# A decoder layer on one core: named slots for transposed tiles, heads in other places among the matmuls, modulation blocks requested a step ahead

## The chip, the cores and the metric

One core of one Trainium2 chip runs the whole kernel. The metric is device time in microseconds (us) of one execution; the median of several runs counts. TensorE (PE) multiplies, VectorE (DVE) and ScalarE (ACT) work on vectors, GpSimd (POOL) makes masks, and SyncE (SP) issues most transfers from memory.

## The reference

One layer on 256 tokens of width 2048, in float32:

```
mod = silu(c) @ w_ada + b_ada              # six pieces: shift, scale, gate, twice
h   = rmsnorm(x) * (1 + s1) + sh1
p   = h @ w_in                             # 2048 x 6160: DA q,k,v; GLA q,k,v,gate, low rank
DA  : 8 heads, softmax(q1 k1) - lam * softmax(q2 k2), causal, ALiBi, then norm
GLA : 4 heads, o_t = q_t S_t,  S_t = diag(a_t) S_(t-1) + k_t v_t, norm, gated
x   = x + g1 * (concat(DA, GLA) @ w_o)
h2  = rmsnorm(x) * (1 + s2) + sh2
x   = x + g2 * ((gelu(conv3(h2 @ w_gate)) * (h2 @ w_val)) @ w_down)   # d_ff = 5632
out = rmsnorm(x) * g_final
```

## The kernel before

Each float32 product is made of three matmuls on a high and a low part of both operands. A unit is two k-tiles (of 128 rows) by 512 columns of a weight, 512 KB: `load_unit` (L110) requests it on SyncE (L122), ScalarE writes the high part `wh` (L125), VectorE the low part `wl` (L126), and TensorE makes 24 matmuls of 256 columns (`b_block`, L144) or 12 of 512 (`a_block`, L178).

The stages in order of time:
1. Start: x is transposed, its norm made, and the modulation of the first two k-tiles.
2. Input projection, in K groups of 2, 2, 4, 4, 4 k-tiles; each group goes over twelve blocks of 512 columns. A block that was begun in an earlier group is copied back into PSUM (L744) and out again (L749).
3. Output projection w_o. It takes the k-tiles 8 to 15 (GLA's heads, `mixT[4]` to `mixT[7]`) first and 0 to 7 (the DA heads, `mixT[0]` to `mixT[3]`) after them.
4. w_up, its K in groups of 4, 4 and 8 k-tiles, then w_down and the last norm.

Beside the units runs other work, written as generators. Background: the modulation blocks (`ada_gen`, L222) request rows of `w_ada` (L243, L246) and add them up on VectorE, weighted by the column of c (`acc`, L256); when a block is full, TensorE sums over partitions (`ps_mod`, L236) and `mod_cols` makes shift and scale (L268 to L271). Then `norm_gen` makes the tiles `hT` (`norm_T`, L281: high part L292 or L296, low part L297). Each unit gives the background a number of steps, `R_K`, `R_WO`, `R_SP`, `R_UP`. Foreground: the GLA heads (`gla`, L683) and the DA heads (`da`, L687), `F_GLA` and `F_DA` steps a unit. A third generator, `setup_consts` (L351), makes masks and constants with casts on VectorE (L374, L401, L415).

A DA head on TensorE is `ps_s` (scores, L577 and L579), `ps_pd` (transposes of the softmax, L607) and `ps_od` (the product with v, L613 to L615). `gla_T` (L553) and `da_T` (L630) transpose the heads' results into `mixT`; `gla_T` is called four times after the whole input projection. Tiles for `hT`, `mixT`, GLA's decay tiles `W` and others come from one pool of eight equal buffers under one name, in turn; PSUM tiles named `ms` have four buffers.

`raw_tile` (L103) gives a buffer for a weight: in the first part a ring of six; from w_up on four `raw2` buffers and four `late` ones, which lie in memory that the first part used. The order of instructions on each engine is that of a scheduler, which takes the program order and its own estimate of times; `keep_in_program_order` fixes an instruction behind the one ahead of it on its engine.

## Time and profile before

| | us |
|---|---|
| three runs | 1346.63, 1340.09, 1338.14 |
| median | 1340.09 |
| profiled execution | 1342.89 |
| its span in the trace | 1341.2 |
| TensorE busy | 1260.1 |
| VectorE busy | 882.0 |
| ScalarE busy | 723.8 |

A busy TensorE may be at its full clock or at half of it; the granted clock of a stretch stands beside its busy time. In brackets behind a row of a timeline stands how long the engine was idle before it, and what ended that.

### The profile page before, as it was taken

How to read it: one execution, taken by the hardware profiler on the slowest of the kernel's cores; microseconds unless marked ns; L12 is line 12 of the kernel's file. 1: busy time of each engine (PE TensorE's matmuls, PEld its weight loads, DVE VectorE, ACT ScalarE, POOL GpSimd, SP SyncE). 2: the span in 40 equal slices, each digit the busy share in tenths (PEclk: the TensorE clock that was granted, in tenths of full speed). 3: DMA queues.
4: the chain of work that ended last, by engine and by line, in shares of the span. 5: the costliest groups of instructions: out<-in, count | busy, mean ns of one | idle time of the engine just before them, and what ended most of it. 6: DMA issues, size and time to landing. Idle time of an engine off the chain costs nothing.

```text
span 1341.2 us, 21471 instructions
## 1 busy us (share of the span) xinstructions
PE 1260.1 (94%) x8556; PEld 1164.6 (87%) x8556; DVE 882.0 (66%) x1135; ACT 723.8 (54%) x937; POOL 30.6 (2%) x79
## 2 busy tenths in 40 slices
...
GB/s 279 298 362 341 307 280 347 268 215 193 177 216 128 201 241 114 180 366 285 285 260 318 237 223 246 231 225 157 210 235 233 233 251 192 173 197 191 190 197 102
DMA packets 159827, 314.58 MB, mean 235 GB/s; under 512 B 12045, under 2 KB 20941, under 8 KB 159726
## 3 DMA queue, kind: packets, MB, share of 16 engines
...
q14 instruction: 34, 0.28, 0.1%
...
## 4 chain that ended last, share of the span: by engine, by line
PE 64%; DMA 19%; DVE 8%; ACT 4%; issue 3%; POOL 2%; DVEq 0%; SPq 0%; POOLq 0%; ACTq 0%
PE ps_h L144 36%; PE ps_d L178 18%; DMA raw_a<-in_w_ada_dram 16%; DVE wl L126 4%; PE ps_mm L144 3%; PE ps_o L144 3%; DVE acc L256 2%; ACT wh L125 2%; DMA raw<-in_w_o_dram 1%; PE ps_mm L178 1%; DMA late<-in_w_up_dram 1%; PE ps_mod L865 1%; DMA late<-in_w_ada_dram 0%; DMA raw<-in_w_in_dram 0%; PE ps_s L579 0%
## 5 line engine op out<-in xcount | busy, mean ns | idle before, releaser
L125 ACT ACTIVATE wh<-raw 128x1024 fp32r<-128x1024 f32 x327 | 344.6, 1057 | 348.9 <-PE ps_d L178 121.4
L126 DVE TENSOR_TENSOR wl<-raw,wh 128x1024 fp32r<-128x1024 f32 x327 | 397.9, 1222 | 194.1 <-ACT wh L125 193.4
L144 PE MATMUL ps_h<-h2T,wh 128*128 128x256 f32 x2816 | 511.5, 285 | 8.1 <-ACT wh L125 8.0
L144 PEld LDWEIGHTS ps_h<-h2T,wh 128*128 128x128 f32 x2816 | 441.9, 193 | 8.2 <-ACT wh L125 8.2
L144 PE MATMUL ps_h<-h2T,wl 128*128 128x256 f32 x1408 | 400.8, 285 | 3.2 <-DVE wl L126 3.2
L256 DVE SCALAR_TENSOR_TENSOR acc<-raw_a,cols,acc 128x1024 f32<-128x1024 f32 (+1 forms) x161 | 192.1, 1194 | 127.5 <-DMA raw_a<-in_w_ada_dram 126.7
L144 PEld LDWEIGHTS ps_h<-h2T,wl 128*128 128x128 f32 x1408 | 271.8, 193 | 4.3 <-DVE wl L126 4.3
L178 PE MATMUL ps_d<-wh,act 128*128 128x512 f32 x704 | 218.1, 390 | 0.8 <-DVE dx L999 0.8
L178 PEld LDWEIGHTS ps_d<-wh,act 128*128 128x128 f32 x704 | 132.2, 188 | 29.5 <-DVE dx L999 1.2
L144 PE MATMUL ps_mm<-hT,wh 128*128 128x256 f32 x768 | 144.1, 289 | 13.2 <-ACT ps_mm L744 5.8
L178 PE MATMUL ps_d<-wl,act 128*128 128x512 f32 x352 | 137.9, 392 | 0.0
L144 PEld LDWEIGHTS ps_mm<-hT,wh 128*128 128x128 f32 x768 | 123.2, 196 | 15.1 <-ACT ps_mm L744 6.6
L178 PE MATMUL ps_mm<-wh,hT 128*128 128x512 f32 x384 | 125.7, 399 | 1.9 <-ACT pj_gq L749 0.6
L144 PE MATMUL ps_mm<-hT,wl 128*128 128x256 f32 x384 | 110.4, 288 | 0.0
L144 PE MATMUL ps_o<-mixT,wh 128*128 128x256 f32 x512 | 98.1, 292 | 7.2 <-DVE mixT L464 5.1
L125 ACT ACTIVATE wh<-late 128x1024 fp32r<-128x1024 f32 x65 | 68.2, 1054 | 58.1 <-PE ps_h L144 35.8
L126 DVE TENSOR_TENSOR wl<-late,wh 128x1024 fp32r<-128x1024 f32 x65 | 79.0, 1221 | 26.7 <-ACT wh L125 23.4
L144 PEld LDWEIGHTS ps_o<-mixT,wh 128*128 128x128 f32 x512 | 82.8, 198 | 8.7 <-DVE mixT L464 5.3
L178 PEld LDWEIGHTS ps_mm<-wh,hT 128*128 128x128 f32 x384 | 73.3, 191 | 19.4 <-ACT ps_mm L744 1.6
L178 PE MATMUL ps_mm<-wl,hT 128*128 128x512 f32 x192 | 76.4, 398 | 2.8 <-DVE wl L126 2.8
L178 PEld LDWEIGHTS ps_d<-wl,act 128*128 128x128 f32 x352 | 66.1, 188 | 14.1 <-issue 0.7
L144 PEld LDWEIGHTS ps_mm<-hT,wl 128*128 128x128 f32 x384 | 75.2, 196 | 0.4 <-issue 0.3
...
## 6 DMA issues: line engine op xcount, KB each, us to landing
raw_a<-in_w_ada_dram SPq DMA_DIRECT2D x142, 512.0 KB, 5.0
raw<-in_w_up_dram SPq DMA_DIRECT2D x111, 512.0 KB, 4.6
raw<-in_w_in_dram SPq DMA_DIRECT2D x96, 512.0 KB, 5.5
raw<-in_w_down_dram SPq DMA_DIRECT2D x88, 512.0 KB, 4.4
late<-in_w_up_dram SPq DMA_DIRECT2D x65, 512.0 KB, 4.9
raw<-in_w_o_dram SPq DMA_DIRECT2D x32, 512.0 KB, 4.8
late<-in_w_ada_dram SPq DMA_DIRECT2D x30, 512.0 KB, 4.4
raw_a<-in_w_ada_dram SPq DMA_DIRECT2D x32, 256.0 KB, 4.8
```

The source lines that it names most:

```text
L125: A.activation(h, raw, AF.Copy)
L126: V.tensor_tensor(l, raw, h, op=ALU.subtract)
L144: PE.matmul(ps[:, m * T:(m + 1) * T], w[:, j, ms], xt[k][:, xx, :], start=(first and k == kts[0] and m % 2 == 0 and i == 0), stop=(last an ...
L178: PE.matmul(ps[:, tb * 512:(tb + 1) * 512], xt[k][:, xx, tsl], w[:, j, :], start=(first and k == kts[0] and i == 0), stop=(last and k == k ...
L256: V.scalar_tensor_tensor(acc, raw[:, j], col, acc, op0=ALU.mult, op1=ALU.add)
L865: PE.matmul(ps_p[:, i:i + 1], pe_rows[k][:, i // 4, i % 4 * P:(i % 4 + 1) * P], cols[:, CK + k:CK + k + 1], start=(k == PE_ROWS[0] and i = ...
```

## The change

- The modulation block of the third K group (4 k-tiles) becomes two of 2 k-tiles, each with its norm (`ADA1`); the input projection drains them half by half. The steps a unit (`R_K`, `R_UP`) and of the DA heads (`F_DA`) are set anew.
- `ada_gen` requests each row one step before it adds it, so each block takes one step more. Its adds, the setup casts and some setup transfers stay in program order; the end of a block and the norms have high priority.
- The pool of eight buffers gets a name for each. GLA's results go into the slots of the decay tiles `W`, and `gla_T` is called inside `gla()`, for heads 0 and 1 after the step of head 2 and for 2 and 3 after the step of head 3, instead of after the input projection.
- `raw_tile` gives the four `raw2` buffers first and the `late` ones after them.
- `spill_o` and `pe_rows` change buffers.

```
+ADA1 = ((2,), (2,), (2, 2), (4,), (4,))
-R_K, R_WO, R_SP, R_UP = (0.95, 1.65, 0.85, 1.1, 0.7), 1.0, 0.75, 0.27
-F_GLA, F_DA = 2.3, 1.8
+R_K, R_WO, R_SP, R_UP = (0.95, 1.85, 0.88, 1.15, 0.75), 1.0, 0.75, 0.28
+F_GLA, F_DA = 2.3, 1.5
...
-    ktp = ctx.enter_context(tc.tile_pool(name="ktp", bufs=8))
+    ktp = ctx.enter_context(tc.tile_pool(name="ktp", bufs=1))
...
         if spare:
-            turn[0] = (turn[0] + 1) % (RAW[0] + len(spare))
-            if turn[0] < len(spare):
-                return spare[turn[0]].rearrange("p (a b) -> p a b", a=shape[1])
+            turn[0] = turn[0] % (RAW[0] + len(spare)) + 1
+            if turn[0] > RAW[0]:
+                return spare[turn[0] - RAW[0] - 1].rearrange("p (a b) -> p a b", a=shape[1])
...
-        for kt in range(0, rows, per):
+        pin = tc.keep_in_program_order
+
+        def load(kt):
             raw = raw_tile([P, per, n], "raw_a")
...
+            return raw
+
+        ahead = load(0)
+        yield
+        for kt in range(0, rows, per):
+            raw, ahead = ahead, load(kt + per) if kt + per < rows else None
...
-                    V.scalar_tensor_tensor(acc, raw[:, j], col, acc, op0=ALU.mult, op1=ALU.add)
+                    pin(V.scalar_tensor_tensor(acc, raw[:, j], col, acc, op0=ALU.mult, op1=ALU.add))
...
-        finish(acc if by_rows else ps)
+        with tc.high_priority():
+            finish(acc if by_rows else ps)
...
-            V.tensor_copy(cmat[:, l], cf)
+            pin(V.tensor_copy(cmat[:, l], cf))
...
-            Wt.append([ktp.tile([P, 4, NTB, P], F32, tag="kt", name=f"W{hd}{i}") for i in range(2)])
+            Wt.append([ktp.tile([P, 4, NTB, P], F32, tag=f"kt{4 + 2 * hd + i}", name=f"W{hd}{i}") for i in range(2)])
...
-        mixT[4 + hd] = kt_tile(f"mixT{4 + hd}")
+        mixT[4 + hd] = kt_tile(f"mixT{4 + hd}", 4 + hd)
...
-        n, k0 = len(kts), kts[0]
-        bg.append(("ada1", ada_gen((0, 1), n * P, k0 * P, mod_cols(s1, sh1, 0, GM, k0, n), get_ps,
-                                   FIRST_PE if g == 0 else ())))
-        bg.append((f"norm{g}", norm_gen(kts)))
+        k0 = kts[0]
+        for n in ADA1[g]:
+            bg.append(("ada1", ada_gen((0, 1), n * P, k0 * P, mod_cols(s1, sh1, 0, GM, k0, n), get_ps,
+                                       FIRST_PE if g == 0 else ())))
+            bg.append((f"norm{k0}", norm_gen(list(range(k0, k0 + n)))))
+            k0 += n
...
             yield from both(*([gla_b(hd - 1)] if hd else []), *([gla_a(hd)] if hd < GLA_HEADS else []))
 
+            for t in {3: (0, 1), 4: (2, 3)}.get(hd, ()):
+                gla_T(t)
+                yield
...
-    steps(5)
+    steps(6)
...
         for i, ks in enumerate(halves):
+            drain(f"norm{ks[0]}")
...
     while len(fg) > 1:
         fstep()
-    for hd in range(GLA_HEADS):
-        gla_T(hd)
     fg.append(da(1))
```

The order of instructions on VectorE at the start, before, from the end of the first modulation block (L268 to L271 make its shift and scale, L297 is the low part of the first `hT`):

```order
36 L365 TENSOR_TENSOR neglam<-lam_136 128x1
37 L256 SCALAR_TENSOR_TENSOR acc<-raw_a,cols,acc 128x512
38 L268 TENSOR_TENSOR sh_131<-ps_mod,bcol 128x2
39 L269 TENSOR_TENSOR s_130<-ps_mod,bcol 128x2
40 L401 CAST cmat<-cf 128x128
41 L366 TENSOR_SCALAR neglam<-neglam 128x1
42 L256 SCALAR_TENSOR_TENSOR acc<-raw_a,cols,acc 128x512
43 L271 SCALAR_TENSOR_TENSOR s_130<-s_130,cols 128x2
44 L401 CAST cmat<-cf 128x128 x2
45 L126 TENSOR_TENSOR wl<-raw,wh 128x1024
47 L401 CAST cmat<-cf 128x128 x2
48 L297 TENSOR_TENSOR hT_293<-xv,hT_293 128x256
```

The same place in the new order (L278 is L268, L281 is L271, L307 is L297, L127 is L126, L265 is L256):

```order
27 L265 SCALAR_TENSOR_TENSOR acc<-raw_a,cols,acc 128x512 x3
28 L374 TENSOR_TENSOR dlam<-dlam 128x128
29 L375 TENSOR_REDUCE lam_136<-dlam 128x2
30 L278 TENSOR_TENSOR sh_131<-ps_mod,bcol 128x2
31 L279 TENSOR_TENSOR s_130<-ps_mod,bcol 128x2
32 L127 TENSOR_TENSOR wl<-raw,wh 128x1024
33 L281 SCALAR_TENSOR_TENSOR s_130<-s_130,cols 128x2
34 L377 TENSOR_TENSOR neglam<-lam_136 128x1
35 L378 TENSOR_SCALAR neglam<-neglam 128x1
36 L307 TENSOR_TENSOR hT_293<-xv,hT_293 128x256
37 L127 TENSOR_TENSOR wl<-raw,wh 128x1024
38 L307 TENSOR_TENSOR hT_293<-xv,hT_293 128x256
```

The casts and the adds of the next block, which stood among them, are no longer there; one `wl` stands between L279 and L281.

TensorE before, from the last heads of DA(0) to the first matmuls of w_o (`ps_o` of L144; `ps_t` are GLA's transposes):

```order
1401 L607 MATMUL ps_pd<-ident,pt 128x128 x2
1402 L613 MATMUL ps_od<-pj_dv_151,pdT 128x128
1403 L614 MATMUL ps_od<-pj_dv_151,pdT 128x128
1404 L615 MATMUL ps_od<-pj_dv_151,pdT 128x128
1405 L607 MATMUL ps_pd<-ident,pt 128x128 x3
1406 L613 MATMUL ps_od<-pj_dv_151,pdT 128x128
1407 L614 MATMUL ps_od<-pj_dv_151,pdT 128x128
1408 L615 MATMUL ps_od<-pj_dv_151,pdT 128x128
1409 L560 MATMUL ps_t<-ident,pj_gg_147 128x128 x8
1410 L560 MATMUL ps_t<-ident,pj_gg_148 128x128 x4
1411 L144 MATMUL ps_o<-mixT_3838,wh 128x256 x2
```

TensorE now: the first of GLA's transposes, in the input projection (`ps_mm` of L145), then, later, where w_o's first half has ended (`mixT_3561` is the last GLA tile) and DA(1) follows (`pj_dq_152`):

```order
1276 L145 MATMUL ps_mm<-hT_2327,wh 128x256 x2
1277 L548 MATMUL ps_o<-pj_gv_146,at 128x256
1278 L549 MATMUL ps_o<-pj_gv_146,at 128x256
1279 L550 MATMUL ps_o<-pj_gv_146,at 128x256
1280 L572 MATMUL ps_t<-ident,pj_gg_147 128x128 x8
1281 L532 MATMUL ps_a<-pj_gq,pj_gk 128x128 x2
```

```order
1662 L145 MATMUL ps_o<-mixT_3561,wh 128x256 x2
1663 L619 MATMUL ps_pd<-ident,pt 128x128
1664 L145 MATMUL ps_o<-mixT_3561,wl 128x256
1665 L619 MATMUL ps_pd<-ident,pt 128x128 x2
1666 L625 MATMUL ps_od<-pj_dv_151,pdT 128x128
1669 L589 LDWEIGHTS identh
1670 L589 MATMUL ps_s_4022<-causal,identh 128x128
1671 L591 MATMUL ps_s_4022<-pj_dk_153,pj_dq_152 128x128
1674 L591 MATMUL ps_s_4022<-pj_dk_153,pj_dq_152 128x256
1681 L619 MATMUL ps_pd<-ident,pt 128x128
1734 L619 MATMUL ps_pd<-ident,pt 128x128 x3
1742 L145 MATMUL ps_o<-mixT_4673,wh 128x256 x3
```

DA(0) stood bare ahead of w_o and DA(1) among its matmuls; now DA(0) stands among the first 384 matmuls of w_o and no `ps_o` stands between the four heads of DA(1) (rows 1666 to 1741).

VectorE at the start of w_up, before (the two L287 are the last parts of the norm, L126 makes `wl`):

```order
538 L297 TENSOR_TENSOR h2T_5334<-xv,h2T_5334 128x512
539 L287 TENSOR_TENSOR xv<-xT,rst_191 128x512 x2
540 L256 SCALAR_TENSOR_TENSOR acc<-late_5369,cols,acc 128x1024
541 L256 SCALAR_TENSOR_TENSOR acc<-raw_a,cols,acc 128x1024
542 L126 TENSOR_TENSOR wl<-late_5370,wh 128x1024
543 L256 SCALAR_TENSOR_TENSOR acc<-raw_a,cols,acc 128x1024
544 L126 TENSOR_TENSOR wl<-late_5370,wh 128x1024
```

and now:

```order
542 L307 TENSOR_TENSOR h2T_5354<-xv,h2T_5354 128x256
543 L297 TENSOR_TENSOR xv<-xT,rst_194 128x512 x2
544 L127 TENSOR_TENSOR wl<-raw,wh 128x1024
545 L265 SCALAR_TENSOR_TENSOR acc<-raw_a,cols,acc 128x1024
546 L127 TENSOR_TENSOR wl<-raw,wh 128x1024
547 L265 SCALAR_TENSOR_TENSOR acc<-raw_a,cols,acc 128x1024
548 L127 TENSOR_TENSOR wl<-late_5399,wh 128x1024
```

The first two units are read from `raw` buffers instead of `late` ones, and no add stands ahead of the first `wl`.

## Rows read from the trace of the kernel before

**Rows 1.** The page: busy time of the engines (share of the span, instructions).

```profile
PE 1260.1 (94%) x8556; PEld 1164.6 (87%) x8556; DVE 882.0 (66%) x1135; ACT 723.8 (54%) x937; POOL 30.6 (2%) x79
```

**Rows 2.** Windows of the span (us): length, busy time and count of instructions of each engine, then the granted clock of TensorE, the share of the transfer engines and the rate.

```profile
12.00:25.00 13.00, 6.01 (x28) 5.55 (x29) 7.27 (x21) 7.32 (x17) 2.53 (x6) 1.00 1.05 314
75.00:100.00 25.00, 24.81 (x162) 22.32 (x160) 20.62 (x18) 18.83 (x20) 0.00 (x0) 1.00 1.03 371
394.00:416.00 22.00, 19.67 (x62) 12.49 (x63) 10.89 (x41) 10.48 (x41) 0.00 (x0) 0.50 0.27 86
425.00:480.00 55.00, 54.99 (x426) 50.40 (x424) 40.37 (x83) 29.31 (x71) 0.00 (x0) 1.00 0.66 210
704.00:731.00 27.00, 24.17 (x197) 23.47 (x196) 17.30 (x16) 14.00 (x15) 0.00 (x0) 1.00 0.96 332
731.00:1087.00 356.00, 356.00 (x2959) 356.00 (x2959) 246.15 (x266) 195.44 (x222) 0.00 (x0) 1.00 0.71 227
```

**Rows 3.** What TensorE waited for, over the whole span: us in total, times, longest.

```profile
PE ps_h L144 <- ACT wh L125: 8.0, 1, 8.0
```

**Rows 4.** Timeline of TensorE at the start: start, length, line, what it writes and reads, count, idle time before and what ended it.

```profile
30.85 1.87 PE L236 MATMUL ps_mod<-ones,acc 128*128 128x1 f32 x8 [3.66 <-DVE acc L256]
36.84 0.79 PE L144 MATMUL ps_mm<-hT,wh 128*128 128x256 f32 x2 [4.12 <-ACT hT L292]
40.94 0.58 PE L144 MATMUL ps_mm<-hT,wh 128*128 128x256 f32 x1 [3.31 <-DVE hT L297]
```

**Rows 5.** Timeline of VectorE in the same stretch.

```profile
32.87 1.26 DVE L126 TENSOR_TENSOR wl<-raw,wh 128x1024 fp32r<-128x1024 f32 x1 [0.26 <-issue]
...
34.83 0.14 DVE L268 TENSOR_TENSOR sh<-ps_mod,bcol 128x2 f32<-128x2 f32 x1
...
35.96 0.19 DVE L271 SCALAR_TENSOR_TENSOR s<-s,cols 128x2 f32<-128x2 f32 x1
...
40.01 0.70 DVE L401 CAST cmat<-cf 128x128 fp32r<-128x128 f32 x2 [0.81 <-POOL cf L393]
40.48 0.41 DVE L297 TENSOR_TENSOR hT<-xv,hT 128x256 fp32r<-128x256 f32 x1
```

**Rows 6.** Timeline of TensorE at the boundary to the third K group.

```profile
114.44 0.79 PE L144 MATMUL ps_mm<-hT,wh 128*128 128x256 f32 x2 [3.91 <-ACT ps_mm L744]
```

**Rows 7.** Timeline of ScalarE there.

```profile
107.61 2.08 ACT L294 ACTIVATE xv<-xv,sh,s 128x256 f32<-128x256 f32 x4
...
111.94 0.63 ACT L296 ACTIVATE hT<-xv 128x512 fp32r<-128x512 f32 x1
...
113.37 1.02 ACT L744 ACTIVATE ps_mm<-pj_gq 128x1024 f32<-128x1024 f32 x1
```

**Rows 8.** Timeline of TensorE from the end of the input projection through the heads of DA(0).

```profile
382.77 0.39 PE L178 MATMUL ps_mm<-wh,hT 128*128 128x512 f32 x1
...
394.03 0.45 PE L607 MATMUL ps_pd<-ident,pt 128*128 128x128 f32 x1 [6.92 <-DVE pt L604]
...
410.38 1.09 PE L607 MATMUL ps_pd<-ident,pt 128*128 128x128 f32 x3
...
413.78 2.77 PE L560 MATMUL ps_t<-ident,pj_gg 128*128 128x128 f32 x12
```

**Rows 9.** The window of one of those heads, columns as in rows 2.

```profile
402.31:410.38 8.07, 7.48 (x22) 4.18 (x22) 3.99 (x17) 3.40 (x15) 0.00 (x0) 0.50 0.23 74
```

**Rows 10.** Timeline of TensorE from w_o's second half to the first matmuls of w_up.

```profile
489.59 0.58 PE L144 MATMUL ps_o<-mixT,wh 128*128 128x256 f32 x1 [5.09 <-DVE mixT L464]
...
542.99 0.59 PE L814 MATMUL ps_q<-sqs,ones 128*128 128x256 f32 x2
...
547.43 7.68 PE L865 MATMUL ps_mod<-cols,raw_p 128*128 128x1 f32 x36
...
564.36 0.58 PE L144 MATMUL ps_h<-h2T,wl 128*128 128x256 f32 x1 [0.46 <-DVE wl L126]
```

**Rows 11.** VectorE's groups by line from 425 to 480 us: count, busy us, mean ns of one, idle time before them and what ended it.

```profile
L126 DVE TENSOR_TENSOR wl<-raw,wh 128x1024 fp32r<-128x1024 f32 x13 | 15.9, 1220 | 1.7 <-ACT wh L125 1.6
L256 DVE SCALAR_TENSOR_TENSOR acc<-raw_a,cols,acc 128x1024 f32<-128x1024 f32 x11 | 14.1, 1284 | 13.5 <-DMA raw_a<-in_w_ada_dram 13.5
```

**Rows 12.** Timeline of VectorE in the heads of DA(0).

```profile
387.72 1.28 DVE L256 SCALAR_TENSOR_TENSOR acc<-raw_a,cols,acc 128x1024 f32<-128x1024 f32 x1 [2.00 <-DMA raw_a<-in_w_ada_dram]
```

**Rows 13.** The page's transfers: engine, count, KB each, median us from issue to landing.

```profile
raw_a<-in_w_ada_dram SPq DMA_DIRECT2D x142, 512.0 KB, 5.0
...
late<-in_w_up_dram SPq DMA_DIRECT2D x65, 512.0 KB, 4.9
...
raw_a<-in_w_ada_dram SPq DMA_DIRECT2D x32, 256.0 KB, 4.8
```

**Rows 14.** What SyncE's queue waited for from 500 to 580 us.

```profile
SPq L243 <- DVE h2T L297: 19.6, 1, 19.6
```

**Rows 15.** Timeline of VectorE at the start of w_up.

```profile
556.35 1.29 DVE L287 TENSOR_TENSOR xv<-xT,rst 128x512 f32<-128x512 f32 x2
560.56 1.28 DVE L256 SCALAR_TENSOR_TENSOR acc<-late,cols,acc 128x1024 f32<-128x1024 f32 x1 [2.92 <-DMA late<-in_w_ada_dram]
```

**Rows 16.** Timeline of SyncE's issues of w_up's units.

```profile
535.24 0.46 SPq L122 DMA_DIRECT2D raw<-in_w_up_dram  x1
...
556.86 0.98 SPq L122 DMA_DIRECT2D late<-in_w_up_dram  x2
```

More of the change, by code (lines that the diff above doesn't have):

```diff
@@ L69, in tile_decoder_layer, with kt_tile @@
     w_down_v = w_down[0].rearrange("(kt p) n -> p kt n", p=P)
-    def kt_tile(name):
-        return ktp.tile([P, 2, 2, T], F32R, tag="kt", name=name)
+    def kt_tile(name, slot):
+        return ktp.tile([P, 2, 2, T], F32R, tag=f"kt{slot}", name=name)
     bg, credit, rate = [], [0.0], [0.0]
@@ L253, in ada_gen @@
                 elif kt + j == 0:
-                    A.activation(acc, raw[:, j], AF.Copy, scale=col)
+                    pin(A.activation(acc, raw[:, j], AF.Copy, scale=col))
                 else:
-                    V.scalar_tensor_tensor(acc, raw[:, j], col, acc, op0=ALU.mult, op1=ALU.add)
+                    pin(V.scalar_tensor_tensor(acc, raw[:, j], col, acc, op0=ALU.mult, op1=ALU.add))
             if not by_rows and (kt + per == rows - n_end or kt + per == rows and not n_end):
@@ L279, in gate_cols, with norm_T @@
         return finish
-    def norm_T(tmp, rst, s_col, sh_col, k0, name, gran):
-        res = kt_tile(name)
+    def norm_T(tmp, rst, s_col, sh_col, k0, name, gran, slot):
+        res = kt_tile(name, slot)
         val = tmp.tile([P, 2, T], F32, tag="xv", name="xv", bufs=2)
@@ L323, in tile_decoder_layer @@
     A.activation(bcol, ps[:, 0:6 * KT], AF.Copy)
-    xtok = [[ktp.tile([P, D // 2], F32, tag="kt", name=f"xtok{tb}{hf}") for hf in range(2)] for tb in range(NTB)]
+    xtok = [[ktp.tile([P, D // 2], F32, tag=f"kt{2 * tb + hf}", name=f"xtok{tb}{hf}") for hf in range(2)]
+            for tb in range(NTB)]
     for tb in range(NTB):
@@ L631, in da_T @@
         b, hb = hp // 2, hp % 2 * 2
-        mixT[hp] = kt_tile(f"mixT{hp}")
+        mixT[hp] = kt_tile(f"mixT{hp}", hp)
         pt = pss.tile([P, 512], F32, tag="ms", name="ps_ot")
@@ L763, in tile_decoder_layer @@
         last = g == len(KG) - 1
-        drain(f"norm{g}")
+        drain(f"norm{kts[0]}")
         rate[0] = R_K[g]
@@ L768, in tile_decoder_layer @@
         if g == len(KG) - 2:
-            nc.scalar.dma_start(out=wlow, in_=w_in_v[:, :, C_LOW:C_LOW + 16])
+            tc.keep_in_program_order(nc.scalar.dma_start(out=wlow, in_=w_in_v[:, :, C_LOW:C_LOW + 16]))
         if last:
@@ L827, in tile_decoder_layer @@
     for nb in range(2):
-        spo.append(prj.tile([P, 1024], F32, tag=("pj_gk", "pj_gq")[nb], name=f"spill_o{nb}"))
+        spo.append(prj.tile([P, 1024], F32, tag=("pj_gg0", "pj_gg1")[nb], name=f"spill_o{nb}"))
         A.activation(spo[nb], po[nb], AF.Copy)
@@ L851, in tile_decoder_layer @@
     pe_rows = {}
-    for k, tag in zip(PE_ROWS, ("gg0", "gg1", "dk0", "dv0")):
+    for k, tag in zip(PE_ROWS, ("gk", "gq", "dk0", "dv0")):
         pe_rows[k] = prj.tile([P, 2, 512], F32, tag=f"pj_{tag}", name="raw_p")
```

25 lines of the change are left out of this document (14 added, 11 removed).

## The prediction, before the changed kernel was run

> **What bounds the kernel now.** I read the busy line first. TensorE is busy 1260.1 of 1341.2 us [rows 1]: little is to be had but the holes of TensorE. Then the windows [rows 2]: from 731 to 1087 us it is fully busy, 2959 matmuls in 356.00 us, so a steady 256-column matmul costs 0.1203 us and a unit of 24 of them 2.9 us. The reader is to see there where this fails: 394 to 416 us runs at a granted clock of 0.50, half of full speed, and 704 to 731 loses 2.8 us. The table of TensorE's waits has as its longest 8.0 us, once, at the start of w_up (`ps_h` for `wh`) [rows 3]. The timelines give the others and say what was queued ahead: 4.1 and 3.3 us for the first `hT` [rows 4, 5], 3.9 us for `ps_mm` [rows 6, 7], 6.9 us in the heads of DA(0) [rows 8, 12], 5.1 us for `mixT` and the 8.0 [rows 10].
>
> The sum is made against the profiled execution, 1342.89 us (span 1341.2 and 1.7 around it). The median of the three runs, 1340.09, is 2.8 lower, and 2.8 comes off at the end.
>
> **Part 1, the start (pinned adds and casts).** TensorE ends the first modulation sums at 32.72 [rows 4] and VectorE adds the bias (L268) only at 34.83, behind `wl` and other work; L271 ends at 36.15, the first matmul comes 0.7 later, at 36.84, and the low half of `hT` (L297), which stood behind casts that wait for GpSimd, at 40.48 [rows 5]; so TensorE goes on at 40.94. In the new order of VectorE no cast is left ahead; L278 follows the reduce directly, one `wl` (1.26) stands between it and L281. If that `wl` ends where the one of before does, at 34.13 [rows 5], the scale is ready near 34.3, TensorE starts near 35.0, and the low half of the first k-tile is there some 1.4 later (two ScalarE steps of about 0.5 and L297's 0.41), near 36.4. Against 40.94 that is 4.5; with nothing in the way of L281 it is 6.3. The lower bound is 3, if only the casts' share goes. I take −5.0. The casts (nine of L401 and seven of L415, 0.35 us each by the two at 40.01) don't vanish: they come later, beside VectorE's waits for transfers, and I cost them at nothing; if that cover is gone they are 16 × 0.35 = 5.6 us of VectorE's queue.
>
> **Part 2, the boundary to the third K group.** At 114.44 TensorE resumes after 3.91 us [rows 6]. The wait is for the copy back into PSUM (L744), which ScalarE begins at 113.37; ahead of it in its queue stands the norm of all four k-tiles, four L294 (2.08 us) and two L296 (0.63 each) [rows 7]. The two halves now have modulation blocks and norms of their own, with 33 background steps needed by the second half and 12 × 0.95 + 12 × 1.85 = 33.6 given (29 and 31.2 before). ScalarE's 3.3 us of norm leave that spot: −3.3, between −3.9 and 0.
>
> **Part 3, what transfers take back.** Sixteen 512 KB requests become 32 of 256 KB, with rows of 1 KB for 2 KB. The nearest stretches are 12 to 25 us, with 1 KB rows (314 GB/s at a share of 1.05), and 75 to 100, mostly 2 KB rows (371 at 1.03) [rows 2]: 299 against 360 GB/s of a full share. 8.39 MB at these is 28.1 against 23.3 us, so +4.8 at most if the transfers bound all of it, and 0 if they don't. A 256 KB request lands in 4.8 us, a 512 KB one in 5.0 [rows 13]: halving it saves nothing. Besides, 75 to 100 us is a full stretch; 8 us less ahead of 114 asks for a share near 1.0 throughout. I take +1.5 for both (0 to +6.4).
>
> [...]
>
> **Part 4, the heads and w_o.** Before: in_proj's last matmul ends at 383.16, w_o's at 542.99 [rows 8, 10], 159.8 us. In it lie three heads of DA(0) without filler (394.03 to 402.31, then 8.07 for the next [rows 8, 9]) and a 6.92 us wait, GLA's transposes, and 5.09 us for `mixT` [rows 8, 10].
> After, by the order: 384 matmuls of w_o with DA(0) between them, then four heads of DA(1) without filler, then the other 384.
> - First stretch: 384 × 0.1203 = 46.2. A head is 7.48 us of TensorE at clock 0.50 [rows 9], 3.74 at full clock; 3.85 heads' worth 14.4. Together 60.6. VectorE has 16 `wl` and 16 `acc` and four heads, 16 × (1.22 + 1.28) [rows 11] + 4 × 3.99 [rows 9] = 56 us: nearly full. I add 2.5 for its waits (1 to 6).
> - Burst: 4 × 8.07 = 32.3, the last two products (410.38 to 413.78 [rows 8], 3.4) and 16 transposes with their copies, 2.8: 38.5.
> - Rest: the same 384 as before from 489.59 to 542.99, 53.4.
> - GLA's 16 transposes go among in_proj's matmuls: 16 × 0.13 = 2.1. Their cost before, 413.78 to 417, stands inside the 159.8.
> Sum 157.1, take −2.7. Its bounds are −9, if the burst runs at the clock of 425 to 480 for half of its heads; +5, if in_proj's last heads push out the end by 2 and the waits reach 6.
>
> Four steps more in `gla()`, at 2.3 a unit, take two units; they are hidden behind in_proj, whose next stretch has GLA's chain in it.
>
> The first DA(0) wait goes since the softmax of head 1 is no longer behind an `acc` that stood 2.00 us for a transfer at 387.72 [rows 12]. What comes late next is the softmax of DA(1) with nothing to fill.
>
> **Part 5, the start of w_up.** TensorE finishes L865 at 555.11 and waits until 563.10, then 564.36 for `wl` [rows 3, 10]. Two units of w_up were requested into `raw` tiles long before, the first at 535.24 [rows 16], but the unit used first has a `late` tile: SyncE's queue stands 19.6 us for L297 [rows 14], that unit is requested at 556.86 [rows 16], and lands 4.9 later [rows 13], near 561.8. In the new ring order the first two units sit in `raw2`, landed. `wl` of unit 0 then follows the two L287 (556.35 to 557.64 [rows 15]) and ends at 558.9: −5.5 against 564.36. Between the two `wl` stands one `acc` from a landed tile (1.28); TensorE has 24 matmuls for that. The third unit is a `late` one still, at 561.9 + 1 + 1.2 = 564; unit 0 and 1 at half clock last until 569. Bounds −6.5 (all at 557.9) and −3 (`acc` waits 2.92 for its transfer, as the one at 560.56 did).
>
> **Part 6, the third w_up group.** Before, 704 to 731 loses 2.8. Now each block has one more step (request ahead); 26 units × 0.75 × 2 = 39 steps are given where 50 and not 47 are needed, so three adds more of 1.28 are drained at once: +1.0, between 0 and +4. Waits of an `acc` on a transfer, of which a drain of nine requests has up to one of 4, are the upper end.
>
> **Sum.** −5.0 − 3.3 + 1.5 − 2.7 − 5.5 + 1.0 = −14.0. 1342.9 − 14.0 = 1328.9; less 2.8, 1326.1 us.
>
> **Rivals.**
> - *Absorbed.* The transfers bind up to 250 us; what parts 1 and 2 give is waited for later. For it: a share of 1.03 at 75 to 100 us [rows 2]. Against: TensorE is busy 24.81 of 25 us in that same stretch, so the transfers keep up there. Part 3 is then +6.4 instead of 1.5, and part 1 gives only 3: 1326.1 + 4.9 + 2 = 1333.
> - *VectorE's queue, the slow side.* Adds pinned in program order stand ahead of `wl` and the softmax, and each waits for its transfer. From 425 to 480 us eleven of them waited 13.5 us [rows 11], 1.23 each, and it cost nothing, since VectorE was busy 40.37 of 55. In the first stretch of part 4 it has 56 us of work in 61: 16 waits of 2.00, as at 387.72, are 32 us, 27 over the cover. Then 1326.1 − 2.5 + 27 = 1350.6. It decides from a mean wait of 0.3 us an add; it is slower than before from about 1.3 up. Against: requests go out a step sooner, so waits should shrink. [...]
> - *The burst only moves and the first unit still waits.* DA(1) now has four bare heads where DA(0) had three; part 4 is then +5 and part 5 nothing: 1326.1 + 7.7 + 5.5 = 1339.
>
> **How the numbers follow.** A measurement of this kernel can tell from no change about 1%, 13.4 us: faster is under 1326.7, slower over 1353.5. The forecast has 0.64, absorbed 0.13, only moved 0.09, VectorE's queue 0.14. The forecast's own range is 1316 to 1334, and I give it 0.69 for under 1326.7, though it lies on the bound, since the bounds of parts 4 and 5 together reach further down (7.3) than up for the likelier of their causes (2.5 for `acc`'s wait). Faster: 0.64 × 0.69 + 0.13 × 0.2 + 0.09 × 0.1 = 0.48. Slower: the half of VectorE's queue in which the waits are over 2.2 us, 0.07. The same: 0.45. The range, 1312 to 1342, leaves out the slow rival and the far tail below.
>
> **What would show it.** Right: first matmul near 35 and no gap over 1 us at 41; no 3.9 us gap near 106; no bare DA(0), a bare stretch of 35 to 40 us at clock 0.50 with the name `ps_s` near 450; the first w_up matmul within 4 us of the last L865-type one. Wrong: L265 waits for transfers with TensorE idle in the first half of w_o; a third-group gap above 6 us; a share of the transfers above 1.0 with TensorE idle between 50 and 110 us.

## The result

The changed kernel is slower: 1360.23 us, median of four runs (1356.82 to 1364.42), against 1340.54 for the kernel before; the ratio is 1.0141, 95% interval 1.0094 to 1.0189. Forecast were 1326.1 us, with a range of 1312 to 1342. The profiled execution is the longest of the four, 1364.42 us with a span of 1362.5, so the sums below speak of 21.3 us between two spans.

The quickest way to see where they went is to read the same marks off both traces: the start of TensorE's first and last matmul of each name. The count of matmuls of each name is the same in both. Matmuls are counted from 0 here. The 432nd of the 1728 `ps_mm` matmuls lies a little past the boundary to the third K group, and the 1344th `ps_h` matmul begins w_up's third K group.

| stretch, between starts of matmuls, us | before | changed | difference |
|---|---|---|---|
| to the first `ps_mm` | 36.8 | 30.6 | −6.2 |
| to the 432nd `ps_mm` | 84.7 | 97.8 | +13.1 |
| to the last `ps_mm` | 261.2 | 248.3 | −12.9 |
| to the last `ps_o` of w_o | 160.1 | 163.8 | +3.7 |
| to the first `ps_h` | 20.2 | 19.3 | −0.9 |
| w_up, K groups one and two | 174.8 | 175.5 | +0.7 |
| w_up, the rest | 349.0 | 373.6 | +24.6 |
| w_down | 243.8 | 243.1 | −0.7 |

The largest entry is in a stretch for which the prediction had no term at all: w_up's third K group and the blocks behind it, in which TensorE was fully busy before [rows 2]. The page of the changed kernel, busy line and the line of the adds:

```profile
PE 1274.9 (94%) x8556; PEld 1170.6 (86%) x8556; DVE 888.7 (65%) x1153; ACT 725.1 (53%) x938; POOL 38.0 (3%) x79
...
L265 DVE SCALAR_TENSOR_TENSOR acc<-raw_a,cols,acc 128x1024 f32<-128x1024 f32 (+1 forms) x173 | 191.1, 1104 | 9.9 <-DMA raw_a<-in_w_ada_dram 7.4
```

TensorE counts as busier than before [rows 1] at the same work, with a mean granted clock of 0.961 for 0.965. The second line holds half of the story: VectorE stands only 9.9 us ahead of its adds, 7.4 of it for rows under way. In the kernel before the page's line, and VectorE's wait for rows in GLA's stretch, 270 to 383 us, were these:

```profile
L256 DVE SCALAR_TENSOR_TENSOR acc<-raw_a,cols,acc 128x1024 f32<-128x1024 f32 (+1 forms) x161 | 192.1, 1194 | 127.5 <-DMA raw_a<-in_w_ada_dram 126.7
```

```profile
DVE acc L256 <- DMA raw_a<-in_w_ada_dram: 24.4, 12, 3.5
```

In that stretch the changed kernel's adds wait for no transfer. That is the good half. The start is earlier than forecast, with a gap of 0.86 us where [rows 4] has 3.31 (timeline of TensorE; the first line is the first modulation sums, which began at 30.85 before):

```profile
27.17 1.05 PE L237 MATMUL ps_mod<-ones,acc 128*128 128x1 f32 x8 [2.31 <-DVE acc L265]
30.58 0.58 PE L145 MATMUL ps_mm<-hT,wh 128*128 128x256 f32 x1 [2.35 <-ACT hT L302]
32.02 0.58 PE L145 MATMUL ps_mm<-hT,wh 128*128 128x256 f32 x1 [0.86 <-DVE hT L307]
```

Windows of the changed kernel (columns as in rows 2):

```profile
25.00:50.00 25.00, 17.31 (x91) 14.85 (x92) 15.87 (x26) 12.67 (x16) 4.54 (x8) 0.86 0.72 234
75.00:100.00 25.00, 22.18 (x145) 19.76 (x144) 17.69 (x24) 18.63 (x21) 0.00 (x0) 1.00 0.84 267
...
825.00:875.00 50.00, 41.41 (x304) 39.92 (x303) 29.87 (x30) 25.59 (x31) 0.00 (x0) 0.86 0.57 190
```

Two things are to be seen. From 75 to 100 us the transfers run at a share of 0.84 and 267 GB/s, where they ran at 1.03 and 371 [rows 2]: in the stretch where the prediction found them full, they are not asked for enough. At the boundary TensorE now waits for weights, and less for the copy back than the 3.91 us of [rows 6] (timeline of TensorE):

```profile
103.09 0.56 PE L179 MATMUL ps_mm<-wh,hT 128*128 128x512 f32 x1 [2.58 <-ACT wh L126]
...
118.15 0.51 PE L145 MATMUL ps_mm<-hT,wh 128*128 128x256 f32 x2 [1.52 <-ACT ps_mm L763]
...
123.90 0.79 PE L145 MATMUL ps_mm<-hT,wh 128*128 128x256 f32 x2 [1.83 <-ACT ps_mm L763]
```

And from 825 to 875 TensorE makes 304 matmuls where 50 us have room for 416 at 0.1203 us each, with the transfers at 0.57: neither is full, so something holds both. Windows of that whole stretch, from the 1344th `ps_h` to the first matmul of w_down, before and then changed, and of two pieces of the changed one:

```profile
737.88:1086.89 349.01, 349.01 (x2914) 349.01 (x2913) 241.33 (x259) 188.68 (x213) 0.00 (x0) 1.00 0.71 227
```

```profile
735.25:1108.88 373.63, 358.59 (x2915) 353.80 (x2913) 239.97 (x258) 184.02 (x206) 0.00 (x0) 0.98 0.66 210
830.40:833.80 3.40, 3.40 (x16) 3.40 (x17) 3.40 (x4) 2.32 (x3) 0.00 (x0) 0.50 0.57 183
854.30:864.60 10.30, 5.62 (x24) 5.33 (x25) 5.83 (x5) 4.51 (x5) 0.00 (x0) 0.50 0.49 155
```

Of the 24.6 us, 15.0 are idle time of TensorE and 9.6 longer busy time. In the two pieces, which lie at waits for `wh` (0.44 us up to 830.39, 6.46 up to 858.52), the clock was granted at 0.50; half of their 9.0 busy us, 4.5 us, is an estimate of what that costs. So with the clock that was granted beside it the second wait cost more than its own 6.46 us: the 24 matmuls of that piece took 5.62 busy us, where 24 at 0.1203 us are 2.9. The table of waits, whole span, its first lines:

```profile
PE ps_h L145 <- ACT wh L126: 17.8, 8, 6.5
PE ps_h L145 <- DVE wl L127: 5.5, 10, 0.8
```

One `wh` wait of 8.0 us was there before [rows 3]; now there are eight, 17.8 us, of which one of 5.9 lies at the start of w_up and six, 9.9 us, in the stretch of the windows.

**The hole at 852 to 858 us, followed back.** TensorE first, then VectorE, then SyncE's queue (timelines; a number in brackets is idle time before the row and what ended it):

```profile
858.52 0.80 PE L145 MATMUL ps_h<-h2T,wh 128*128 128x256 f32 x2 [6.46 <-ACT wh L126]
```

```profile
846.94 1.00 DVE L955 SCALAR_TENSOR_TENSOR y<-ps_h,nconv,y 128x255 f32<-128x255 f32 x2 [4.11 <-ACT y L953]
...
851.84 1.00 DVE L955 SCALAR_TENSOR_TENSOR y<-ps_h,nconv,y 128x255 f32<-128x255 f32 x2 [0.63 <-ACT y L953]
852.76 1.27 DVE L265 SCALAR_TENSOR_TENSOR acc<-late,cols,acc 128x1024 f32<-128x1024 f32 x1
```

```profile
842.86 0.37 SPq L123 DMA_DIRECT2D late<-in_w_up_dram  x1
854.06 0.37 SPq L123 DMA_DIRECT2D late<-in_w_up_dram  x1
```

SyncE issues nothing from 843.2 to 854.06. The request at 854.06 wants a `late` buffer that holds a modulation row; the add that reads that row ends at 854.03, 0.03 us earlier. The row itself was requested at 831.81 and had landed by about 837, by the median of 5.1 us of its kind: the add was late, not the row. It is late because it is pinned behind the convolution's steps (L955) in VectorE's queue, and these wait for TensorE to end the block that feeds them. TensorE ended it, and then had no weights, because every later request stood behind the one that waited. SyncE's waits from 825 to 880 us name it, and behind them stand those for adds from 780 to 1110:

```profile
SPq L123 <- DVE acc L265: 22.4, 5, 10.8
SPq L123 <- DVE wl L127: 20.7, 13, 2.9
```

```profile
SPq L123 <- DVE acc L265: 34.8, 18, 10.8
```

**The start of w_up.** The first two units do lie in `raw` buffers now, yet the first `ps_h` came only 0.9 us sooner after w_o's end. SyncE's waits from 500 to 580 us, ScalarE's timeline and SyncE's:

```profile
SPq L246 <- ACT acc L263: 20.6, 1, 20.6
```

```profile
551.80 0.61 ACT L306 ACTIVATE h2T<-xv 128x512 fp32r<-128x512 f32 x1
552.32 1.13 ACT L263 ACTIVATE acc<-raw_a,cols 128x1024 f32<-128x1024 f32 x1
```

```profile
553.48 0.37 SPq L246 DMA_DIRECT2D raw_a<-in_w_ada_dram  x1
553.90 0.46 SPq L123 DMA_DIRECT2D raw<-in_w_up_dram  x1
```

The same pattern again. The first row of a modulation block was requested ahead into a buffer of the first part; its first add, L263 on ScalarE, is pinned behind the norm (L306) and runs at 552.32; the new buffers lie in that memory, and SyncE's queue stands 20.6 us until 553.48. In the kernel before the first w_up unit was requested at 535.24 [rows 16], here at 553.90.

### The profile page after: what moved, and what is told of

Its sections match the earlier page's. It is cut to its first block, busy times and chain, and to the rows that moved or that the text cites. A ratio compares the mean times of both kernels' runs of the same rounds, so it can differ in the third digit from the quotient of the medians.

```text
span 1362.5 us, 21533 instructions
## 1 busy us (share of the span) xinstructions
PE 1274.9 (94%) x8556; PEld 1170.6 (86%) x8556; DVE 888.7 (65%) x1153; ACT 725.1 (53%) x938; POOL 38.0 (3%) x79
## 4 chain that ended last, share of the span: by engine, by line
PE 68%; DMA 15%; DVE 7%; ACT 7%; issue 3%; SPq 0%; ACTq 0%; POOL 0%; POOLq 0%; DVEq 0%
PE ps_h L145 29%; PE ps_d L179 18%; DMA raw<-in_w_in_dram 7%; PE ps_mm L145 5%; PE ps_o L145 5%; DVE wl L127 4%; PE ps_mm L179 4%; ACT wh L126 4%; DMA raw<-in_w_up_dram 3%; DMA raw<-in_w_o_dram 2%; PE ps_s L591 2%; DMA late<-in_w_up_dram 2%; DVE acc L265 1%; PE ps_mod L237 1%; PE ps_a L532 1%
## 5 line engine op out<-in xcount | busy, mean ns | idle before, releaser
L127 DVE TENSOR_TENSOR wl<-raw,wh 128x1024 fp32r<-128x1024 f32 x329 | 401.5, 1224 | 297.9 <-ACT wh L126 289.3
L126 ACT ACTIVATE wh<-raw 128x1024 fp32r<-128x1024 f32 x329 | 346.8, 1057 | 406.1 <-PE ps_d L179 118.1
L145 PE MATMUL ps_h<-h2T,wh 128*128 128x256 f32 x2816 | 515.1, 286 | 17.8 <-ACT wh L126 17.8
L145 PEld LDWEIGHTS ps_h<-h2T,wh 128*128 128x128 f32 x2816 | 444.4, 194 | 20.0 <-ACT wh L126 20.0
L145 PE MATMUL ps_h<-h2T,wl 128*128 128x256 f32 x1408 | 402.4, 286 | 5.5 <-DVE wl L127 5.5
L145 PEld LDWEIGHTS ps_h<-h2T,wl 128*128 128x128 f32 x1408 | 273.1, 194 | 7.8 <-DVE wl L127 7.7
L265 DVE SCALAR_TENSOR_TENSOR acc<-raw_a,cols,acc 128x1024 f32<-128x1024 f32 (+1 forms) x173 | 191.1, 1104 | 9.9 <-DMA raw_a<-in_w_ada_dram 7.4
L145 PE MATMUL ps_mm<-hT,wh 128*128 128x256 f32 x768 | 144.2, 288 | 8.8 <-ACT ps_mm L763 4.8
L145 PEld LDWEIGHTS ps_mm<-hT,wh 128*128 128x128 f32 x768 | 122.8, 195 | 11.2 <-ACT ps_mm L763 5.7
L127 DVE TENSOR_TENSOR wl<-late,wh 128x1024 fp32r<-128x1024 f32 x63 | 76.6, 1223 | 62.2 <-ACT wh L126 62.0
L145 PE MATMUL ps_mm<-hT,wl 128*128 128x256 f32 x384 | 110.3, 288 | 2.8 <-DVE wl L127 2.8
L126 ACT ACTIVATE wh<-late 128x1024 fp32r<-128x1024 f32 x63 | 65.8, 1055 | 70.0 <-PE ps_h L145 34.7
L145 PE MATMUL ps_o<-mixT,wh 128*128 128x256 f32 x512 | 96.5, 289 | 6.5 <-ACT ps_o L878 2.8
L145 PEld LDWEIGHTS ps_o<-mixT,wh 128*128 128x128 f32 x512 | 81.7, 196 | 8.3 <-ACT ps_o L878 2.9
L145 PEld LDWEIGHTS ps_mm<-hT,wl 128*128 128x128 f32 x384 | 74.9, 195 | 3.6 <-DVE wl L127 3.6
```

Source lines behind the costliest of these rows:

```text
L126: A.activation(h, raw, AF.Copy)
L127: V.tensor_tensor(l, raw, h, op=ALU.subtract)
L145: PE.matmul(ps[:, m * T:(m + 1) * T], w[:, j, ms], xt[k][:, xx, :], start=(first and k == kts[0] and m % 2 == 0 and i == 0), stop=(last an ...
L265: pin(V.scalar_tensor_tensor(acc, raw[:, j], col, acc, op0=ALU.mult, op1=ALU.add))
```

## The experiments

Twelve kernels, each timed beside the kernel before on the same chip; each ratio is to that. First, the two suspects of w_up, one taken away at a time and both added to the kernel before. "From w_up on" is the condition `RAW[0] == 4`, so the program ahead of it is unchanged.

**Adds not pinned from w_up on.**

```
-        pin = tc.keep_in_program_order
+        pin = tc.keep_in_program_order if RAW[0] == 6 else lambda i: i
```

> The changed kernel, except that from w_up on the weighted adds (acc) are no longer kept in program order; everything ahead of w_up as in the changed kernel. w_up (first ps_h to first ps_d) takes 523.7 us before and 549.1 changed. Theory 1 (the pin: an add whose row landed long ago stands behind the convolution's steps on VectorE, its buffer comes free late, and SyncE's queue stands with all later weight requests behind it): w_up falls to 524 to 530 us, no TensorE gap over 2 us between 830 and 1060, the kernel 1335 to 1342. Theory 2 (the request a step ahead holds a buffer of the ring by itself, whatever the order of the adds): w_up stays at 543 to 549. Theory 3 (the new turn of the ring, raw buffers ahead of the late ones, or the rate 0.28): stays at 545 to 549.

1337.74 us, ratio 0.9985 (0.9969 to 1.0001). w_up took 524.1 us, 25.0 less than in the changed kernel. SyncE's waits for adds from 780 to 1110 us are many and short:

```profile
SPq L123 <- DVE acc L265: 20.2, 15, 1.7
```

The longest is 1.7 us, where it was 10.8, and TensorE has no wait for `wh` from 800 to 1080 us; the kernel before has 20.1 us, 15 times, at most 1.7, in its w_up from 758 us on. The pin is needed for the loss. A long stand of the queue was not harmful as such: in the kernel before it once stood 10.9 us for `wl` between 850 and 950 us, with TensorE busy 100.00 of the 100 us at a clock of 1.00. What sets the two apart was not followed.

**No request ahead from w_up on.**

```
-        ahead = load(0)
+        late_load = RAW[0] == 4
+        ahead = None if late_load else load(0)
...
-            raw, ahead = ahead, load(kt + per) if kt + per < rows else None
+            if late_load:
+                raw = load(kt)
+            else:
+                raw, ahead = ahead, load(kt + per) if kt + per < rows else None
```

> The changed kernel, except that from w_up on a modulation row is requested in the step that adds it, not a step before; the adds stay pinned in program order and each block keeps its count of steps. Theory 1 (the pin): the late add still holds a buffer, w_up stays above 538 us. Theory 2 (the request ahead holds the buffer): w_up falls to 524 to 530 us. Theory 3 (turn of the ring, rate): stays at 545 to 549. Should pin and request be needed together, e1 and e2 both fall to about 525.

1332.21 us, ratio 0.9948 (0.9932 to 0.9965). w_up 518.7 us, pins kept. So the request ahead is needed too: either edit taken away ends the loss, as the last sentence of the expectation allowed. Of the two, the pin without the request is the better by 5.4 us, all of it in the second K group (84.6 us against 90.0): the stretch with the drain at its end, where the kernel before lost 2.8 us [rows 2].

**Both, added to the kernel before, from w_up on.** The pinned, requested-ahead `ada_gen` with `up = RAW[0] == 4` in its two conditions; old turn, old rates.

> The kernel before, with only two things added, from w_up on: a row is requested a step ahead, and the adds are kept in program order (old turn of the ring, old rates). Theories 1 and 2: w_up grows from 523.7 to 540 us or more, with SyncE's queue waiting for acc by more than 5 us at a time. Theory 3: w_up stays at 522 to 527 us.

1354.52 us, ratio 1.0102 (1.0074 to 1.0129). w_up 534.8, 11.0 more than before, and less than the 540 expected (its first two K groups are 4.7 quicker, the rest is 15.7 slower); w_down 247.6 and 3.8 more. SyncE and TensorE from 780 to 1110 us:

```profile
SPq L122 <- DVE acc L270: 33.8, 19, 9.1
```

```profile
PE ps_h L144 <- ACT wh L125: 7.6, 3, 6.7
```

The same wait appears, and with it a loss, without any other part of the change. Why it costs 15 us here and 25 in the changed kernel, which has the other turn of the ring and a rate of 0.28, isn't taken apart further.

**The heads' part alone**, on the kernel before: named slots, `gla_T` inside `gla()`, `F_DA` 1.5, the moved buffers.

> The kernel before with the heads' part of the change alone: named slots, gla_T inside gla(), F_DA 1.5, the moved buffers of spill_o and the last rows; no request ahead, no pins, no split blocks, old rates. From the end of the input projection to the end of w_o it is 160.1 us before (382.8 to 542.9) and 163.9 changed (376.6 to 540.5). If the heads' rearrangement is worth what was predicted, w_o ends at 540 or earlier, and DA(1) stands bare for 35 to 40 us; if the bare heads cost more than predicted by themselves, w_o ends at 545 or later; if the changed kernel lost it to held weight requests (SyncE stood 38.3 us for a step of DA(1) there), no such wait is seen here and w_o ends near 537.

1341.74 us, ratio 1.0010 (0.9993 to 1.0027). w_o ends at 541.5; from the last `ps_mm` to it 160.0 us against 160.1. The rearrangement is worth nothing by itself: the bare heads are DA(1)'s instead of DA(0)'s, as the rival said that the burst only moves. Windows of this kernel, the first half of w_o with DA(0), the bare heads, and the rest:

```profile
381.90:455.00 73.10, 69.69 (x485) 60.45 (x483) 54.59 (x109) 36.01 (x90) 0.00 (x0) 0.93 0.75 246
455.00:490.90 35.90, 28.61 (x104) 19.52 (x103) 18.37 (x59) 15.66 (x56) 0.00 (x0) 0.57 0.32 103
490.90:541.60 50.70, 49.54 (x408) 48.77 (x407) 30.96 (x53) 21.78 (x35) 0.00 (x0) 1.00 0.38 126
```

and the same three stretches of the changed kernel:

```profile
377.00:438.40 61.40, 61.40 (x467) 55.57 (x465) 45.63 (x90) 32.88 (x74) 0.00 (x0) 1.00 0.74 246
438.40:480.40 42.00, 34.48 (x124) 22.95 (x122) 18.18 (x70) 18.12 (x70) 0.00 (x0) 0.58 0.12 38
480.40:540.70 60.30, 52.95 (x409) 51.28 (x408) 42.38 (x63) 21.43 (x35) 0.00 (x0) 0.96 0.51 167
```

Then, the request ahead, the adds' pins, the split block and the turn, in the whole kernel.

**No request ahead anywhere** (pins, split, slots and turn as changed).

```
-        ahead = load(0)
         yield
         for kt in range(0, rows, per):
-            raw, ahead = ahead, load(kt + per) if kt + per < rows else None
+            raw = load(kt)
```

> The changed kernel with no modulation row requested ahead anywhere; pins, split blocks, slots, ring turn and rates as changed. In the changed kernel SyncE's queue stood 20.6 us, to 553.48, for the first add (ACT acc L263) of a block whose row had been requested ahead into memory of the first part, and with it the first two units of w_up; from the end of w_o to the first ps_h it took 19.3 us (before 20.2; with no ahead from w_up on alone 18.2, the same wait being there for 19.0). Theory H (held buffer): that wait goes, the distance falls to 13 to 15 us, w_up takes 517 to 525, the kernel 1322 to 1330. Rival: something else keeps the requests back (the pins), the distance stays at 18 to 20. The stretch from the 288th to the 432nd ps_mm matmul, 30.3 us before and 38.3 changed: theory H 30 to 33; rival (split blocks: more and smaller requests) 35 to 38.

1316.88 us, ratio 0.9815 (0.9783 to 0.9847): this one edit turns 1.4% slower into 1.9% faster. From w_o's end to the first `ps_h` 14.6 us, as theory H put it; TensorE no longer waits for weights there:

```profile
536.65 0.77 PE L145 MATMUL ps_h<-h2T,wh 128*128 128x256 f32 x2 [1.20 <-DVE bcol L886]
```

In the two runs that keep pins and requests ahead up to w_up the distance is 18.1 and 19.6. From the 288th to the 432nd `ps_mm` it took 34.2, between both expectations (before 30.3, changed 38.3). The kernel is faster than expected by 5 us or more: the input projection ends at 362.9, 13.7 ahead of the changed kernel.

**No add pinned anywhere** (`pin = lambda i: i` in `ada_gen`, which frees the adds on VectorE and the first add on ScalarE; requests ahead and the setup's pins stay).

> The changed kernel with no add pinned anywhere (requests still a step ahead, setup casts still pinned). If the pin is what costs in w_up and the request ahead harmless, it is the fastest form, 1325 to 1332, and the stretch from the 288th to the 432nd ps_mm matmul returns to 30 to 33 us. If the request ahead costs by itself ahead of w_up, that stretch stays at 35 or more, the distance from w_o's end to the first ps_h stays at 18 to 20, and the kernel ends at 1335 to 1342, as with unpinned adds from w_up on alone (1337.7). First ps_mm: 30.6 changed, 36.8 before; if the adds' pin makes the earlier start, it goes back to 33 or later, if the setup casts' pin does, it stays at 30 to 32.

1328.24 us, ratio 0.9902 (0.9865 to 0.9939). The first 432 matmuls are the best of all (ending at 112.0; 288th to 432nd 29.5), the first at 30.4, so the earlier start comes from the setup's pins. Windows of this kernel:

```profile
25.00:50.00 25.00, 20.61 (x102) 18.43 (x103) 22.14 (x34) 15.67 (x19) 4.14 (x7) 0.80 1.03 341
```

The transfers run at a share of 1.03, where the changed kernel has 0.72 in the same stretch: with the adds pinned the requests thin out, which fits buffers that come free late. The cost comes later: w_o took 166.9 us and w_up's second group 98.5, with rows awaited again by VectorE (101.8 us in all), and 14.0 us from w_o's end to `ps_h` was not the 18 expected.

**The third group's modulation in one block again**, on the kernel without requests ahead (`ADA1` with `(4,)`; the `drain` of the second half, which has no norm of its own then, goes too).

> As the run without any request ahead, but the third K group's modulation in one block of 4 k-tiles again (512 KB requests, one drain). If the split makes the loss at that boundary, the stretch from the 288th to the 432nd ps_mm matmul is 30 to 32 us here and 35 or more with the split; if the split is good for the 3.3 us of the prediction, it is 3 us longer here than with it.

1312.51 us, ratio 0.9783 (0.9754 to 0.9811), the lowest median, though its interval overlaps that of the run with the split. The boundary stretch is 31.2 us against 34.2 with the split, yet both end the input projection at 362.9. The split loses 3 us there and gets them back. The medians lie 4.4 us apart, the two profiled executions 2.1: w_o takes 156.4 against 159.1 and the way to the first `ps_h` 12.2 against 14.6, w_up 526.7 against 523.7, with the same lines in both.

**The old turn of the ring**, on the kernel without requests ahead.

> As the run without any request ahead, but with the old turn of the ring, late buffers first. The prediction gave the turn 5.5 us: then w_o's end to the first ps_h is 18 to 20 us here and 13 to 15 with the new turn. If the turn is worth nothing, both agree within 1 us.

1316.13 us, ratio 0.9809 (0.9776 to 0.9842). From w_o's end to the first `ps_h` 18.5 against 14.6, so the new turn does bring 3.9 us; w_up then takes 519.2 against 523.7, and the whole is the same. What the first units gain is given back within w_up.

Last, single parts on the kernel before, to see which one gained in the input projection.

**Adds pinned, nothing else.**

```
-                    A.activation(acc, raw[:, j], AF.Copy, scale=col)
+                    tc.keep_in_program_order(A.activation(acc, raw[:, j], AF.Copy, scale=col))
...
-                    V.scalar_tensor_tensor(acc, raw[:, j], col, acc, op0=ALU.mult, op1=ALU.add)
+                    tc.keep_in_program_order(V.scalar_tensor_tensor(acc, raw[:, j], col, acc, op0=ALU.mult, op1=ALU.add))
```

> The kernel before with one thing added: every weighted add (acc) is kept in program order. No request ahead, nothing else. Theory V (VectorE stood in front of its queue for a row still under way, 126.7 us in all, 24.4 of them from 270 to 383 us, with GLA's work behind it; the pin puts an add behind work that the row needs to land): that wait falls below 30 us, the input projection from the 432nd ps_mm matmul to its end goes from 261.2 us to 245 to 250, and the kernel to 1322 to 1332. Rival (that gain came from the new rates and the setup, not from the adds): the stretch stays at 258 to 262 and the kernel at 1336 or more.

1323.14 us, ratio 0.9885 (0.9857 to 0.9912), from the order of two lines alone. The page's line of the adds is as theory V has it:

```profile
L256 DVE SCALAR_TENSOR_TENSOR acc<-raw_a,cols,acc 128x1024 f32<-128x1024 f32 (+1 forms) x161 | 191.6, 1190 | 9.1 <-DMA raw_a<-in_w_ada_dram 6.0
```

VectorE waits 6.0 us for rows instead of 126.7; from the 432nd `ps_mm` to the last it takes 246.7 us and not 261.2.

**One step ahead, nothing pinned.** The generator of the change with `pin = lambda i: i`, and `steps(6)`.

> The kernel before with each modulation row requested one step ahead and nothing pinned. With the adds unpinned in the changed kernel VectorE still stood 101.8 us for rows, so theory V gives little here: wait for rows 60 to 115 us, the stretch from the 432nd ps_mm matmul to the end 252 to 260, the kernel 1330 to 1340. If the request ahead by itself holds buffers harmfully, as in w_up with the pin, w_up takes 530 us or more and the kernel is over 1345.

1363.19 us, ratio 1.0178 (1.0148 to 1.0208). Expected was a small gain; it is the slowest of the twelve, and the alternative in the expectation came true: w_up 530.5. The adds:

```profile
L264 DVE SCALAR_TENSOR_TENSOR acc<-raw_a,cols,acc 128x1024 f32<-128x1024 f32 (+1 forms) x158 | 188.2, 1192 | 139.0 <-DMA raw_a<-in_w_ada_dram 138.0
```

A request a step ahead doesn't even shorten VectorE's wait for rows (138.0 against 126.7). It loses 8.3 us from the first to the 432nd `ps_mm`, 8.9 in w_o and 6.7 in w_up. The changed kernel with its adds unpinned also requests ahead without pinned adds, and is faster than before; which of its other parts makes up for this isn't shown.

**The setup's pins alone** (casts, first transfers, `wlow`).

> The kernel before with only the setup casts, the first setup transfers and wlow kept in program order. The prediction put 5 us on the start (first ps_mm at 36.8 before, 30.6 changed, TensorE going on at 40.9 before). If it is the casts: first ps_mm at 30 to 33 and the 432nd matmul 4 to 7 us earlier than 121.5. If the transfers take it back: the 432nd matmul at 120 to 122. The kernel 1333 to 1340.

1331.88 us, ratio 0.9932 (0.9906 to 0.9958), 1 us better than the range expected. TensorE at the start:

```profile
30.76 0.58 PE L144 MATMUL ps_mm<-hT,wh 128*128 128x256 f32 x1 [2.20 <-ACT hT L292]
32.20 0.58 PE L144 MATMUL ps_mm<-hT,wh 128*128 128x256 f32 x1 [0.86 <-DVE hT L297]
```

The whole earlier start is theirs, 30.8 against 36.8, and the 432nd matmul comes at 113.6 and not 121.5: what was gained at the start is not taken back by the transfers. From there to the last `ps_mm` it takes 252.8 us, 8.4 less than before, while VectorE still waits for rows in the last 113 us of the projection, 253 to 366.5 us:

```profile
DVE acc L256 <- DMA raw_a<-in_w_ada_dram: 21.2, 13, 3.1
```

**No request ahead, no split, old turn.**

> As the run without any request ahead and without the split block (1312.5 us), with the old turn of the ring. The turn alone made no difference to the whole kernel (1316.1 and 1316.9): expected 1311 to 1315, w_o's end to the first ps_h 17 to 19 us against 12.2, w_up 519 to 522 against 526.7. Rival (the two add up): 1309 or less, or 1317 or more.

1314.39 us, ratio 0.9807 (0.9779 to 0.9835), the same as with the new turn (1312.51). w_o's end to `ps_h` 18.3, w_up 518.2: as expected, the turn moves time and saves none.

## Why the prediction was wrong, point by point

- **Part 1, the start: right in mechanism, the rest of the gain not forecast.** From the end of the first modulation sums to the first matmul it is 2.36 us for 4.12 [rows 4], and from there to the second 1.44 for 4.10: together −4.4, where −5.0 was taken. But the prediction held the sums' end fixed at 32.72, and they now end at 28.22, 4.5 us earlier; so the first matmul came at 30.58 and not near 35. At the point that the part used, 40.94, the gain is 8.9 us, beyond its bounds; that the table's −6.2, taken at the first matmul, lies near −5.0 is luck. The setup's pins alone give all of it. The casts are also shorter than the 0.35 us read off one row: 0.26 and 0.23 in the median, some 4 us in place of 5.6.
- **Parts 2 and 3, boundary and transfers: wrong in sign.** −3.3 and +1.5 were forecast up to there; the stretch from the first to the 432nd matmul grew by 13.1. The step that failed is "I take +1.5 for both": it priced how the transfers run, smaller requests and a full stretch, and took the requests themselves as given. They were not: from 25 to 50 us the transfers ran at a share of 0.72 with the adds pinned and 1.03 without. The stretch is 97.8 us with pins and requests ahead, 89.4 with the pins alone and 81.6 with the requests ahead alone (84.7 before), so the whole loss takes both. On the kernel before, each alone costs: adds pinned 6.3 us (91.0), the request ahead 8.3 (93.0); why the latter costs there and not in the changed kernel isn't shown. Part 2's own wait did shrink, from 3.91 us to 1.52 (the 384th `ps_mm`), but 1.83 more stand at the 408th and TensorE waits 2.58 us for `wh` ahead of it. The split by itself makes the boundary 3.0 us longer (34.2 against 31.2), and without it that wait is 1.49 us all the same, so that the split shortens it isn't shown.
- **A term that was missing: VectorE's waits for rows.** The prediction read the 13.5 us of [rows 11] and found that they cost nothing there, beside w_o's matmuls. In GLA's stretch such waits (24.4 us from 270 to 383) stood in VectorE's queue with GLA's own steps behind them. Pinning the adds, by itself, ends the waits and takes 14.5 us off the stretch; the changed kernel has −12.9. How much of that is the waits' is not shown: the setup's pins alone give −8.4 with the waits still there.
- **Part 4, the heads: the order came as forecast, the gain did not.** −2.7 was forecast with bounds from −9 to +5; the rearrangement alone gives −0.1, the changed kernel +3.7, without requests ahead −1.0 and −3.7. The term that was mis-sized differs: by the rearrangement alone the first stretch takes 73.1 us for 60.6 + 2.5, the burst 35.9 for 38.5 and the rest 50.7 for 53.4; in the changed kernel 61.4, 42.0 and 60.3. There the rest, taken as unchanged, is the worst term: TensorE is idle for 7.4 us of it, 2.7 of them for `wh`, after SyncE's queue had stood 38.3 us in the burst. Where rows are requested ahead before w_up, w_o took 162.2 to 169.0 us, elsewhere 155.1 to 161.4. How the request delays it was not followed further: without it SyncE's queue stands 34.3 us there too.
- **Part 5, the start of w_up: the step "in the new ring order the first two units sit in `raw2`, landed" failed.** They were in `raw2` and not landed: SyncE's queue stood 20.6 us for a pinned add of a row requested ahead. Without requests ahead the distance fell by 5.6, the forecast being 5.5, but only 3.9 of it is the turn's, so that the figures agree is in part luck; and the kernel still gained nothing from the turn, since w_up gave it back.
- **Part 6: right in number,** +0.7 for +1.0 over the two groups. That it is the three more adds isn't shown: without the request ahead from w_up on each block keeps its extra step, and the second group is 5.4 us shorter.
- **The term that decided, w_up's third group and the blocks behind it, +24.6, was nowhere in the sum.** The prediction says of the pins that they come "in program order", of the requests that "requests go out a step sooner, so waits should shrink". The second is the step that failed: it never puts pin and request beside the queue that both feed, where a buffer is taken a step earlier and released by an add that may not move forward. VectorE's waits for rows did shrink, to 7.4 us, and SyncE's waits for adds, up to 10.8 us at a time, came in their place; either edit taken away ends the loss. The rival on VectorE's queue came nearest, a loss from pinned adds and 1350.6 us; but it looked for adds that wait for rows in the first half of w_o, where TensorE was busy 61.4 of 61.4 us, and what happened was rows that wait for adds.
- **The other rivals:** the heads' burst only moved, as one said. The start was not absorbed by full transfers: with the setup's pins alone the 432nd matmul still comes 7.9 us earlier.
